# Pairing the second half's forget gate and query: two Strassen units, a seventh buffer pair, and scalings on ScalarE

## The chip, the core and the metric

The kernel runs on one core of a Trainium2 chip. The engines that matter here are PE (TensorE, the matmul engine; its weight loads are counted apart as PEld), DVE (VectorE), ACT (ScalarE), POOL (GpSimd) and SP (SyncE, whose queue issues the weight transfers). The metric is the device time of one execution in microseconds (us), as the median of several runs.

## The reference

A single layer of a hybrid block over 256 tokens of width 2048: a gated short convolution beside a gated linear recurrence with 8 heads of 128, a gated merge, an output projection and a per-token embedding gate, all in float32.

```python
h = rmsnorm(x, norm_mix_g[i])
u = h @ w_in[i]
c_g, b_g, xa, za, q, fl, iv, og, ga, gb = jnp.split(u, split_idx, axis=-1)
ya = b_g * causal_dwconv3(c_g * xa, conv_w[i]) * jax.nn.silu(za)
...
log_f = jnp.logaddexp(jnp.log(jnp.maximum(lb, LB_FLOOR)),
                      jnp.log1p(-lb) + jax.nn.log_sigmoid(flf))
kk = (1.0 - lb) * jax.nn.sigmoid(-flf)
o = hgrn2_chunked(jax.nn.silu(q), kk, iv, log_f)          # reshaped to heads
...
m = jax.nn.sigmoid(ga) * (ya @ w_a_out[i]) + jax.nn.sigmoid(gb) * (yb @ w_b_out[i])
x = x + m @ w_o[i]
gate = jax.nn.sigmoid(rmsnorm(x, ple_norm_g[i]) @ w_ple_gate[i])
x = x + gate * (p[i] @ w_ple_proj[i])
```

The column blocks `q`, `fl` (the forget gate, `f` in the kernel), `iv` and `og` are 1024 wide and belong to the recurrence. `log_f` equals the logarithm of `lb + (1 - lb) * sigmoid(fl)`; the kernel computes it so, per head, with `one` = 1 - lb and `low` = lb as per-partition columns, since features lie on the partitions there.

## The kernel before, in words

**Products.** Every float32 matmul is made of three products of a high and a low part: `x_hi w_hi + x_hi w_lo + x_lo w_hi`. The weights come in chunks of 128 x 1024 values, called positions here and numbered through the whole program (`pos`). For each position ACT makes the high part (`whi`, L166: a copy to the matmul type) and DVE the low part (`wlo`, L167: raw minus `whi`). PE then issues 12 products of 128 x 512. L1258 is the matmul of a plain group, L1280 that of a pair.

**Groups.** The program runs group after group; a group is a block of 512 output columns, and a block of 1024 input columns is handled as halves 0 and 1. For the first half: `f`, then `QV` (query and value as a pair), `og`, `c`, `xa`, `za`, `b`. For the second half: `f` at positions 72 to 79, `q` at 80 to 87, and `VG` (value and output gate as a pair) at 88 to 109, then `c`, `xa`, `za`, `b`. After that come the merge gates `G0` and `GG`, the branch projections `A` and `B`, the output projection (`OO`, a pair, then two plain groups `O`), and the gate of the embedding `PG`, `GP`. In all 342 positions.

**Pairs and units.** A pair makes two groups at once after a program such as `INNER`, a tuple of entries. `(g, c)` stands for two plain positions for group g, from k-chunk c on (`(2, c)` for one position each for both groups). `("S", c)` is a Strassen unit of four positions (parts 0 to 3) that need 6, 3, 6 and 6 products, 21 in place of 24. For a unit DVE forms sums of raw weights after part 0's split (`combine_weights`, L181, L184, L185; part 1 is then only 512 wide), and sums of inputs are kept as `form`s. Since a unit leaves its results in eight banks, the function `sums` adds these up to the two outputs (L845, after a copy by ACT, L858); it starts the work on the first output as soon as it is complete, then the second.

**What sets the order.** Each engine runs its instructions strictly in the program's order, which is that of the code. At each position PE's products are written, the casts and splits run ahead by `ahead(pos)` positions (LEAD = 3, and one more for each additional buffer pair where the rule in `ahead` allows it), and every active epilogue (a generator, such as `ep_f`) advances by one step: one step for each plain position, one for every second part of a unit. In the regions where extra pairs are named, further order constraints keep casts, splits and steps in that order.

**Buffers.** `whi` and `wlo` rotate through four pairs of the pool `wp`; in some regions of the program (`MORE`) there are one or two extra pairs, made of tiles that happen to be unused there. With n extra pairs a position takes an extra one where `pos % (4 + n) < n`, otherwise the next of the four. So a position's number decides which earlier position must be finished before its cast. Region "inner" has two extra pairs, around `QV` and around `VG`. Raw weights come by transfers of SP's queue, three buffers deep; `turned` turns a gate to the layout of features on partitions by way of DRAM and a transpose on DVE (L354).

**The forget gate.** `ep_f` takes the product of `f`, scales it (L362), turns it, takes two sigmoids on ACT (L400, L402), applies the per-head scalings on DVE (L407: times `one` plus `low`; L414: times `one`), four each per half, loads the table for the logarithm, takes logarithms (L424, L425, L428) and makes a running sum on DVE (the scan, L434); two short operations follow (L439, L440).

Of the kernel before, what the change touches and what calls it, by code (L numbers as in the profile page):

```python
# [40 lines left out]

GATES = ("S", 0), (0, 2), ("S", 1), (1, 2), ("S", 4), (0, 6), ("S", 5), (1, 6)
OPENING = (0, 2), (0, 4), ("S", 0), (0, 6), ("S", 1), (1, 2), (1, 4), (1, 6)
INNER = (0, 4), ("S", 0), (0, 6), ("S", 1), (2, 3), ("S", 2), (1, 4), (1, 6)
# [11 lines left out]
def hybrid_kernel(ctx, tc, xT, x, pT, prm, gfin, masks, w_in, w_a, w_b, w_o, w_pg, w_pp, out):  # L56
# [117 lines left out]
    def combine_weights(pos):  # L174

        b = load(pos).rearrange("p i (k c) -> p (i k) c", k=2)
        pool, tag, n = ("tmp2", "t2", 2) if more(pos) in ("gates", "last") else ("tmp3", "t2", 1)
        if more(pos) in ("inner", "first"):
            pool, tag, n = "tmp1", ("both", "aoff")[unit_of[pos] // 2 % 2], 1
        t2 = half[unit_of[pos]] = pools[pool].tile([P, CW], F32, tag=tag, bufs=n, name=nm("t2"))  # L180
        nc.vector.tensor_tensor(  # L181
            out=b[:, 0:4:3, :], in0=b[:, 0:3:2, :], in1=b[:, 3:4, :].to_broadcast([P, 2, CW]), op=ALU.subtract
        )
        nc.vector.tensor_tensor(out=t2, in0=b[:, 2, :], in1=b[:, 0, :], op=ALU.add)  # L184
        nc.vector.tensor_tensor(out=b[:, 1, :], in0=b[:, 1, :], in1=t2, op=ALU.subtract)  # L185
# [27 lines left out]
    for gi, (kind, j, w, g, op, *program) in enumerate(groups):  # L213
# [4 lines left out]
        for n, (u, c) in enumerate(program[0]):  # L218
# [10 lines left out]
    LEAD = 3  # L229
# [26 lines left out]
    inner = [of_kind(kind) for kind in ("QV", "VG")]  # L256
    inner = range(inner[0][0] - 3, inner[0][-1] + 1), range(inner[1][0] - 6, inner[1][-1] + 1)

    def more(pos):

        return "gates" if pos in gates else "last" if pos in last else "outer" if pos in outer else "first" if pos in g0 else "inner" if any(pos in at for at in inner) else None

# [132 lines left out]
    def ep_f(j, psum):  # L395
# [9 lines left out]
        for h in range(4):  # L405
            s = slice(h * T, (h + 1) * T)
            nc.vector.tensor_scalar(  # L407
                out=sg[:, s], in0=sg[:, s], scalar1=one[:, h : h + 1], scalar2=low[:, h : h + 1],
                op0=ALU.mult, op1=ALU.add,
            )  # L410
        yield
        for h in range(4):
            s = slice(h * T, (h + 1) * T)
            nc.vector.tensor_scalar(  # L414
                out=kT[:, s], in0=sn[:, s], scalar1=one[:, h : h + 1], scalar2=None, op0=ALU.mult
            )
        yield
# [484 lines left out]
    def ep_out(j, e, left):  # L902
# [6 lines left out]
        yield from sums(e, left, lambda: (t4(), t4()), then)  # L909

    def ep_a(j, psum):
        g = state["ga", j]
# [406 lines left out]
    for pos, (gi, c) in enumerate(steps[:last_group]):  # L1319
# [53 lines left out]
        if program:  # L1373
# [4 lines left out]
            if c == (min(n for n, (u, _) in enumerate(program) if u == "S"), 0) and kind not in ("G0", "OO"):  # L1378
                active.append({"GG": ep_pair, "GP": ep_gates_late, "QV": ep_inner, "VG": ep_inner}[kind](j, banks, left))
            pair_products(c, program, opname)  # L1380
# [160 lines left out]
```

## Time and profile before

| | |
|---|---|
| Time, median of 3 runs | 808.21 us (807.93 to 808.41) |
| Profiled execution: time, span | 809.07 us, 807.3 us |
| Granted TensorE clock, mean | 0.996 |
| PE busy | 99% of the span |
| DVE busy | 85% |
| ACT busy | 61% |
| POOL busy | 12% |

The profiled execution is one run of the program; the times quoted from timelines are microseconds from its span's start. A row of a timeline has start, duration, engine, line, operation, output and inputs, shapes and a count; in brackets how long the engine was idle before, and what released it. A row of the chain that ended last has start, duration, engine, output and line. With PE busy 99% of the span, a change can save at most the products that it removes and the few gaps, and it can add whatever time it makes PE wait.

### The profile page before, as it was taken

To read this page: it belongs to the slowest core of one execution; us is meant where nothing else is said; L and a number is where in the kernel's file an instruction comes from. 1 tells how busy PE (TensorE), PEld (TensorE's weight loads), DVE (VectorE), ACT (ScalarE), POOL (GpSimd) and SP (SyncE) were. 2 spreads that over 40 slices of the span, in tenths; PEclk is the share of its full clock that TensorE was granted. 3 is DMA by queue.
4 is the path that set the end of the run, shared out by engine and by line. 5 is a ranking of instruction groups with operands and counts; after the bars stand their busy time and mean duration, and the time that the engine had idled before them with its cause. 6 is when DMAs were issued, how large, how long until landed. Compare 5 with 4: busy or idle time off the path is not lost.

```text
span 807.3 us, 11113 instructions
## 1 busy us (share of the span) xinstructions
PE 798.0 (99%) x4169; PEld 662.3 (82%) x4169; DVE 685.1 (85%) x798; ACT 492.1 (61%) x662; POOL 95.4 (12%) x74
## 2 busy tenths in 40 slices
PE   9999999999999999999999999999999999999995
PEld 7888888888888888888888888888888888887885
DVE  5968897966779987978998998998998988859995
ACT  6967565575656665586674564564565556746562
POOL 0000145300000054300001000000100000002032
PEclk9999999999999999999999999999999999999998
DMA  9899855747676755667584775775875669877542
GB/s 345 295 335 319 268 174 203 237 167 241 240 261 190 261 183 201 209 211 257 189 307 158 227 275 171 239 264 179 275 266 196 208 246 348 327 236 281 205 173 104
DMA packets 50309, 191.20 MB, mean 237 GB/s; under 512 B 5712, under 2 KB 15184, under 8 KB 36304
## 3 DMA queue, kind: packets, MB, share of 16 engines
q1 hardware_dynamic: 50112, 190.24, 68.4%
q8 instruction: 32, 0.52, 0.2%
q10 hardware_dynamic: 144, 0.26, 0.1%
q14 instruction: 21, 0.17, 0.1%
HBM read 175.80 MB, written 14.68 MB: 236 GB/s over the span
## 4 chain that ended last, share of the span: by engine, by line
PE 82%; DVE 10%; issue 2%; DMA 2%; ACT 2%; SPq 0%; POOL 0%; ACTq 0%; POOLq 0%; DVEq 0%
PE g L1258 48%; PE g L1280 25%; PE s L1280 6%; DVE wlo L167 5%; DMA raw<-in_w_pg 2%; ACT whi L166 1%; DVE raw L181 1%; DMA raw<-in_w_o 1%; PE s L1258 1%; PE s L504 1%; DVE t L845 1%; PE s L1131 1%; DVE t L184 1%; DVE t L1017 0%; DVE t L354 0%
## 5 line engine op out<-in xcount | busy, mean ns | idle before, releaser
L167 DVE TENSOR_TENSOR wlo<-raw,whi 128x1024 fp32r<-128x1024 f32 (+1 forms) x320 | 390.2, 1243 | 92.2 <-ACT whi L166 89.4
L166 ACT ACTIVATE whi<-raw 128x1024 fp32r<-128x1024 f32 (+1 forms) x320 | 325.8, 1047 | 175.8 <-PE g L1258 98.3
L1258 PE MATMUL g<-whi,xl 128*128 128x512 f32 (+1 forms) x464 | 177.1, 382 | 0.3 <-DVE xl L311 0.3
L1258 PE MATMUL g<-whi,xh 128*128 128x512 f32 (+1 forms) x464 | 177.4, 383 | 0.0
L1258 PE MATMUL g<-wlo,xh 128*128 128x512 f32 (+1 forms) x464 | 177.1, 382 | 0.0
L1280 PE MATMUL g<-whi,xl 128*128 128x512 f32 x316 | 122.9, 389 | 0.0
L1280 PE MATMUL g<-wlo,xh 128*128 128x512 f32 x316 | 122.9, 389 | 0.0
L1280 PE MATMUL g<-whi,xh 128*128 128x512 f32 x316 | 122.6, 389 | 0.0
L1258 PEld LDWEIGHTS g<-whi,xl 128*128 128x128 f32 x464 | 87.2, 188 | 17.6 <-DVE xl L311 0.8
L1258 PEld LDWEIGHTS g<-whi,xh 128*128 128x128 f32 x464 | 87.2, 188 | 17.0 <-ACT xh L310 0.3
L1258 PEld LDWEIGHTS g<-wlo,xh 128*128 128x128 f32 x464 | 87.3, 188 | 16.8
L166 ACT ACTIVATE whi<-t 128x512 fp32r<-128x512 f32 x25 | 15.8, 632 | 92.1 <-DVE t L184 92.1
L1280 PEld LDWEIGHTS g<-whi,xl 128*128 128x128 f32 x316 | 59.3, 188 | 12.4
L1280 PEld LDWEIGHTS g<-whi,xh 128*128 128x128 f32 x316 | 59.3, 188 | 12.3
L1280 PEld LDWEIGHTS g<-wlo,xh 128*128 128x128 f32 x316 | 59.3, 188 | 12.3
L927 POOL TENSOR_TENSOR t<-ga,gb 128x512 f32<-128x512 f32 x6 | 10.6, 1790 | 188.0 <-issue 118.1
L181 DVE TENSOR_TENSOR raw<-raw 128x1024 f32<-128x1024 f32 x25 | 31.5, 1261 | 0.6
L1258 PE MATMUL g<-whi,yaTh 128*128 128x512 f32 (+1 forms) x74 | 28.2, 388 | 0.0
L1258 PE MATMUL g<-wlo,yaTh 128*128 128x512 f32 (+1 forms) x74 | 27.9, 383 | 0.0
L1258 PE MATMUL g<-whi,yaTl 128*128 128x512 f32 (+1 forms) x74 | 27.9, 383 | 0.0
L1258 PE MATMUL g<-whi,mh 128*128 128x512 f32 x64 | 24.8, 391 | 0.1
L1258 PE MATMUL g<-whi,ml 128*128 128x512 f32 x64 | 24.9, 389 | 0.0
(309 smaller groups left out, 1117.0 us busy)
## 6 DMA issues: line engine op xcount, KB each, us to landing
raw<-in_w_in SPq DMA_DIRECT2D x68, 1024.0 KB, 5.0
raw<-in_w_in SPq DMA_DIRECT2D x37, 512.0 KB, 5.1
raw<-in_w_o SPq DMA_DIRECT2D x12, 1024.0 KB, 6.5
raw<-in_w_pg SPq DMA_DIRECT2D x12, 1024.0 KB, 6.4
raw<-in_w_in SPq DMA_DIRECT2D x38, 256.0 KB, 5.1
turn<-t SPq DMA_DIRECT2D x72, 128.0 KB, 2.8
t<-turn SPq DMA_DIRECT2D x18, 512.0 KB, 5.2
raw<-in_w_a SPq DMA_DIRECT2D x8, 1024.0 KB, 5.6
```

The costliest lines, as they stand in the source:

```text
L166: a = nc.scalar.activation(out=hi[:, s], in_=src[:, s], func=AF.Copy)
L167: v = nc.vector.tensor_tensor(out=lo[:, s], in0=src[:, s], in1=hi[:, s].bitcast(F32), op=ALU.subtract)
L181: nc.vector.tensor_tensor(out=b[:, 0:4:3, :], in0=b[:, 0:3:2, :], in1=b[:, 3:4, :].to_broadcast([P, 2, CW]), op=ALU.subtract)
L184: nc.vector.tensor_tensor(out=t2, in0=b[:, 2, :], in1=b[:, 0, :], op=ALU.add)
L504: nc.tensor.matmul(heads(bk)[r, h, c if at is None else slice(at, at + 32)], key(h)[:, r], query(h)[:, c], start=True, stop=True, tile_pos ...
L845: nc.vector.tensor_tensor(out=out, in0=x, in1=y, op=ALU.add)
L927: (nc.vector if j == 3 else nc.gpsimd).tensor_tensor(out=spread(m, t), in0=blocks(ga[:, s]), in1=blocks(gb[:, s]), op=ALU.add)
L1131: nc.tensor.matmul(wb[:m, :n], *ones, start=True, stop=True)
L1258: nc.tensor.matmul(psum, a, b, start=first and n == 0, stop=last and n == 2)
L1280: nc.tensor.matmul(banks[name], x, y[:, s], start=k == total[name] and i == 0, stop=k == 1 and i == 2)
```

## The change

It does four things.

1. Groups `f` and `q` of the second half become a pair `FQ` with the program `SECOND`: six plain entries of two positions and two Strassen units, 20 positions (72 to 91) in place of 16. `ep_second` passes the first output to `ep_f` and the second to `ep_q`. `VG` moves to 92 to 113, and all later positions rise by four (the whole program has 346).
2. A new region "wide", from four positions before `VG` to its end, has a third extra pair made of the tiles `og` and `cv`, so seven pairs in all; `ahead` has a case for it. Region "inner" now reaches from two positions before `FQ` to the start of "wide".
3. In `ep_f` the eight scalings of each half leave DVE (L407, L414) and become activations on ACT (L415 with scale and bias as per-partition columns, L421 with a scale).
4. The input sums for `VG`'s third unit (`third`) start at a place counted from "wide".

Lines of the new kernel lie a little lower: L166 becomes L167, L167 becomes L168, L400 becomes L408, L845 becomes L850, L1280 becomes L1296.

```diff
+SECOND = (0, 2), (0, 4), ("S", 0), (0, 6), ("S", 1), (1, 2), (1, 4), (1, 6)
...
-        if more(pos) in ("inner", "first"):
+        if more(pos) in ("inner", "wide", "first"):
             pool, tag, n = "tmp1", ("both", "aoff")[unit_of[pos] // 2 % 2], 1
...
-        elif (kind, j) in (("iv", 0), ("og", 1)):
+        elif (kind, j) == ("f", 1):
+            groups.append(("FQ", j, w_in, n, "hT", SECOND))
+        elif (kind, j) in (("iv", 0), ("og", 1), ("q", 1)):
             continue
...
+        "wide": (
+            (("tmp1", "X"), ("tmp1", "X")), (("tmp1", "a"), ("tmp1", "y")), (("tmp1", "og"), ("tmp1", "cv")),
+        ),
...
-    inner = range(inner[0][0] - 3, inner[0][-1] + 1), range(inner[1][0] - 6, inner[1][-1] + 1)
+    wide = range(inner[1][0] - 4, inner[1][-1] + 1)
+    inner = range(inner[0][0] - 3, inner[0][-1] + 1), range(of_kind("FQ")[0] - 2, wide[0])
+    tied.append(wide)
...
-            nc.vector.tensor_scalar(
-                out=sg[:, s], in0=sg[:, s], scalar1=one[:, h : h + 1], scalar2=low[:, h : h + 1],
-                op0=ALU.mult, op1=ALU.add,
+            nc.scalar.activation(
+                out=sg[:, s], in_=sg[:, s], func=AF.Identity, scale=one[:, h : h + 1], bias=low[:, h : h + 1]
             )
...
-            nc.vector.tensor_scalar(
-                out=kT[:, s], in0=sn[:, s], scalar1=one[:, h : h + 1], scalar2=None, op0=ALU.mult
-            )
+            nc.scalar.activation(out=kT[:, s], in_=sn[:, s], func=AF.Identity, scale=one[:, h : h + 1])
...
+    def ep_second(j, e, left):
+
+        def then(q, g):
+            after = (ep_q if q else ep_f)(j, [g[:, A], g[:, B]])
             next(after)
             active.append(after)
+
+        yield from sums(e, left, lambda: (t4(), t4()), then)
...
-        while n < len(MORE[at]) and more(pos + LEAD + n + 1) == at and (at == "gates" or more(pos + LEAD - 2 * n) == at):
+        while n < len(MORE[at]) and more(pos + LEAD + n + 1) == at and (
+            at == "gates" or more(pos + LEAD - 2 * n) == at or at == "wide" and n < 2
+        ):
             n += 1
...
-        if pos == inner[1][0] - 8:
+        if pos == wide[0] - 10:
```

The order of instructions shows where things stand. On ACT, in the kernel before, the forget gate of the second half comes among the casts of `VG`'s first unit (`whi_2210` to `whi_2288` are its parts 0 to 3; L400 and L402 are the sigmoids, L370 a part of q's activation).

```order
L166 ACTIVATE whi_2210<-raw_2152 128x1024 [waits DMAHW4_49,DVE_49,PE_49]
L400 ACTIVATE t_367_2208<-t_366_2206 128x1024 [waits DMAHW6_49,DMAHW7_49,DMAHW1_49,DVE_49]
L402 ACTIVATE t_366_2206<-t_366_2206 128x1024 [waits Activation_49]
L166 ACTIVATE whi_2240<-t_370_2214 128x512 [waits DVE_49,PE_49]
L166 ACTIVATE whi_2260<-raw_2152 128x1024 [waits DVE_49,PE_49]
L370 ACTIVATE t_377_2276<-g_2115,r1r_615 128x512 [waits PE_49]
L370 ACTIVATE t_377_2276<-g_2116,r1r_615 128x512 [waits PE_49]
L166 ACTIVATE whi_2288<-raw_2152 128x1024 [waits DMAHW6_49,DMAHW5_49]
L424 ACT_TABLE_LOAD
L424 ACTIVATE t_385_2306<-t_367_2208 128x4x128 [waits DVE_49]
```

On ACT, in the changed kernel, the same work comes among the casts of `VG`'s second unit (`whi_2366` is its part 0, position 100; `whi_2385` to `whi_2404` are parts 1 to 3, and `whi_2422` is position 104).

```order
L167 ACTIVATE whi_2366<-raw_2264 128x1024 [waits DMAHW3_49,PE_49,Activation_49]
L408 ACTIVATE t_393_2304<-t_392_2302 128x1024 [waits DVE_49]
L378 ACTIVATE t_399_2327<-t_363_2141,r1r_615 128x512 x2
L410 ACTIVATE t_392_2302<-t_392_2302 128x1024 [waits Activation_49]
L415 ACTIVATE t_393_2304<-t_393_2304,lc_54_330,lc_55_331 128x256 x4
L421 ACTIVATE kT_2340<-t_392_2302,lc_55_331 128x256 [waits Activation_49]
L421 ACTIVATE kT_2340<-t_392_2302,lc_55_331 128x256 x3
L167 ACTIVATE whi_2385<-t_408_2370 128x512 [waits DVE_49,PE_49]
L167 ACTIVATE whi_2393<-raw_2264 128x1024 [waits DVE_49,PE_49]
L167 ACTIVATE whi_2404<-raw_2264 128x1024 [waits DMAHW6_49,DMAHW4_49,PE_49]
L429 ACT_TABLE_LOAD
L429 ACTIVATE t_421_2416<-t_393_2304 128x4x128 [waits Activation_49]
```

The batch has moved back by one unit and two plain entries, and the eight scalings have joined it, ahead of the casts of parts 1 to 3.

On DVE, in the changed kernel, the transpose of the forget gate (L362) follows the split of position 100 (`wlo_2367`), and the scan (L439) stands between the splits of 105 and 106.

```order
L168 TENSOR_TENSOR wlo_2367<-raw_2264,whi_2366 128x1024 [waits DMAHW3_49,Activation_49]
L362 STREAM_TRANSPOSE t_392_2302<-t_375_2197 128x4x8x32 [waits DMAHW5_49]
L182 TENSOR_TENSOR raw_2264<-raw_2264 128x2x512 [waits DMAHW6_49,DMAHW4_49,DVE_49]
...
L168 TENSOR_TENSOR wlo_2423<-raw_2324,whi_2422 128x1024 [waits DMAHW7_49,Activation_49]
L168 TENSOR_TENSOR wlo_2441<-raw_2324,whi_2440 128x1024 [waits DMAHW0_49,PE_49,Activation_49]
L439 SCALAR_TENSOR_TENSOR b_2456<-carry,t_421_2416 128x1024 [waits Pool_49]
L168 TENSOR_TENSOR wlo_2460<-raw_2381,whi_2459 128x1024 [waits DMAHW1_49,Activation_49]
...
L444 COPY tot_2457<-b_2456 128x4x2
L445 TENSOR_TENSOR tot_2457<-b_2456,lfl_2417 128x4x2
L362 STREAM_TRANSPOSE qT_2333<-t_400_2328 128x4x8x32 [waits DMAHW1_49]
L168 TENSOR_TENSOR wlo_2486<-raw_2381,whi_2485 128x1024 [waits Activation_49]
```

On DVE, in the kernel before, the scan (L434) stood one unit earlier: behind the splits of `VG`'s (0, 6) and of S1's part 0 (`wlo_2344`), ahead of S1's weight sums (L181).

```order
L167 TENSOR_TENSOR wlo_2314<-raw_2188,whi_2313 128x1024 [waits DMAHW7_49,Activation_49]
L167 TENSOR_TENSOR wlo_2333<-raw_2188,whi_2332 128x1024 [waits Activation_49]
L167 TENSOR_TENSOR wlo_2344<-raw_2230,whi_2343 128x1024 [waits DMAHW0_49,PE_49,Activation_49]
L434 SCALAR_TENSOR_TENSOR b_2359<-carry,t_385_2306 128x1024 [waits Pool_49]
L181 TENSOR_TENSOR raw_2230<-raw_2230 128x2x512 [waits DMAHW2_49,DMAHW1_49,DVE_49]
```

So the scan and the transposes of f and q have moved behind one more unit of `VG`.

On ACT at the start of the output projection `OO`, the kernel before casts parts 2 and 3 of the first unit (`whi_5564`, `whi_5585`) and the position behind them so:

```order
L166 ACTIVATE whi_5531<-t_976_5527 128x512 [waits DVE_49,PE_49,Activation_49]
L166 ACTIVATE whi_5564<-raw_5440 128x1024 [waits DVE_49,PE_49,Activation_49]
L166 ACTIVATE whi_5585<-raw_5440 128x1024 [waits DMAHW6_49,DMAHW5_49]
L166 ACTIVATE whi_5589<-raw_5489 128x1024 [waits DMAHW7_49,PE_49,Activation_49]
L784 ACTIVATE Sm_5608<-t_980_5551 128x512 [waits DVE_49]
```

and the changed kernel, at the same place with positions four higher, so:

```order
L167 ACTIVATE whi_5567<-t_992_5563 128x512 [waits DVE_49,PE_49,Activation_49]
L167 ACTIVATE whi_5600<-raw_5476 128x1024 [waits DVE_49,PE_49,Activation_49]
L167 ACTIVATE whi_5621<-raw_5476 128x1024 [waits DMAHW1_49,DMAHW2_49,PE_49,Activation_49]
L167 ACTIVATE whi_5625<-raw_5525 128x1024 [waits DMAHW3_49]
L789 ACTIVATE Sm_5644<-t_996_5587 128x512 [waits DVE_49]
```

The same five instructions stand in the same order, but their buffers have rotated: the cast of part 3 now waits for PE, and the cast behind it does not.

More of the change, by code (lines that the diff above doesn't have):

```diff
@@ L256, in hybrid_kernel @@
     inner = [of_kind(kind) for kind in ("QV", "VG")]
-    inner = range(inner[0][0] - 3, inner[0][-1] + 1), range(inner[1][0] - 6, inner[1][-1] + 1)
+    wide = range(inner[1][0] - 4, inner[1][-1] + 1)
+    inner = range(inner[0][0] - 3, inner[0][-1] + 1), range(of_kind("FQ")[0] - 2, wide[0])
+    tied.append(wide)
     def more(pos):
-        return "gates" if pos in gates else "last" if pos in last else "outer" if pos in outer else "first" if pos in g0 else "inner" if any(pos in at for at in inner) else None
+        return "gates" if pos in gates else "last" if pos in last else "outer" if pos in outer else "first" if pos in g0 else "wide" if pos in wide else "inner" if any(pos in at for at in inner) else None
     TOKENS, NORM, FORMS, MASKS = 10, 13, 5, 30
@@ L909, in ep_out @@
         yield from sums(e, left, lambda: (t4(), t4()), then)
+    def ep_second(j, e, left):
+        def then(q, g):
+            after = (ep_q if q else ep_f)(j, [g[:, A], g[:, B]])
+            next(after)
+            active.append(after)
+        yield from sums(e, left, lambda: (t4(), t4()), then)
     def ep_a(j, psum):
@@ L1378, in hybrid_kernel @@
             if c == (min(n for n, (u, _) in enumerate(program) if u == "S"), 0) and kind not in ("G0", "OO"):
-                active.append({"GG": ep_pair, "GP": ep_gates_late, "QV": ep_inner, "VG": ep_inner}[kind](j, banks, left))
+                active.append({"GG": ep_pair, "GP": ep_gates_late, "QV": ep_inner, "VG": ep_inner, "FQ": ep_second}[kind](j, banks, left))
             pair_products(c, program, opname)
```

## The prediction

> **What bounds the kernel now.** I read the page's first part, the chain that ended last, the table of windows around the change, and then the timelines of PE, ScalarE (ACT) and VectorE (DVE) there.
>
> ```profile
> PE 798.0 (99%) x4169; PEld 662.3 (82%) x4169; DVE 685.1 (85%) x798; ACT 492.1 (61%) x662; POOL 95.4 (12%) x74
> ```
> ```profile
> 177.53 62.58 PE g L1258 x276
> ...
> 240.10 5.44 PE g L1280 x24
> ```
> ```profile
> 200.00:220.00 20.00, 20.00 (x90) 16.54 (x90) 14.75 (x19) 11.15 (x16) 0.11 (x1) 1.00 0.78 270
> 240.00:260.00 20.00, 20.00 (x90) 16.57 (x89) 18.05 (x24) 13.79 (x18) 0.53 (x1) 1.00 0.49 158
> 260.00:280.00 20.00, 19.97 (x89) 16.21 (x88) 19.28 (x21) 12.56 (x15) 0.00 (x0) 1.00 0.74 263
> ```
>
> PE is full, so only two things change the time: the number of products, and stretches in which PE is left without a split weight. One product takes 62.58 / 276 = 0.2267 us. In the windows (length; then PE, PEld, DVE, ACT, POOL; granted clock; DMA share; GB/s) DVE has 5 us to spare at 200 to 220, 2.0 at 240 to 260, 0.7 at 260 to 280. DVE is the second bound exactly where the changed groups hand over to VG. VG starts at 240.10; FQ's 20 positions need 6 products less than the 16 of f and q, so after the change VG would start at 240.10 - 1.36 = 238.74.
>
> ```profile
> 268.05 0.39 PE L1280 MATMUL g<-whi,xh 128*128 128x512 f32 x1
> ...
> 268.80 0.39 PE L1280 MATMUL s<-whi,form 128*128 128x512 f32 x1
> ```
>
> These two starts are two products apart and should differ by 0.45, not 0.75: PE already loses 0.30 us in VG's third unit, S2.
>
> **The change, part by part.** *Products.* One unit has 21 in place of 24, so two save 6: -1.36 us. The 0.30 of S2 goes too, since what follows counts S2's delay from its nominal place.
>
> *The gate batch, moved into VG.* Before, f's last product runs at 177.53 + (84 + 96) x 0.2267 = 218.3 (7 and 8 positions of 12), and the work on its gates stands among the casts of VG's first unit S0, 6 to 12 us before PE reaches them (S0 starts at 240.10 + 5.44 = 245.54):
>
> ```profile
> 235.75 1.06 ACT L400 ACTIVATE t<-t 128x1024 f32<-128x1024 f32 x1 [1.00 <-DMA raw<-in_w_in]
> ...
> 241.31 1.24 ACT L370 ACTIVATE t<-g,r1r 128x512 f32<-128x512 f32 x2
> ...
> 243.52 1.28 ACT L424 ACT_TABLE_LOAD   x1
> 244.81 0.63 ACT L424 ACTIVATE t<-t 128x512 f32<-128x512 f32 x1
> ...
> 245.97 2.94 ACT L166 ACTIVATE whi<-raw 128x1024 fp32r<-128x1024 f32 x3
> ```
> ```profile
> L407 DVE TENSOR_SCALAR t<-t,lc,lc x8: 406/408/414, 77.9 to 240.2; 128x256 f32<-128x256 f32 x8
> L414 DVE TENSOR_SCALAR kT<-t,lc x8: 334/348/555, 81.5 to 241.9; 128x256 f32<-128x256 f32 x8
> L434 DVE TENSOR_TENSOR_SCAN b<-carry,t x2: 2276/2280/2283, 87.4 to 250.5; 128x1024 f32<-128x1024 f32 x2
> ```
> ```profile
> 205.75 1.69 ACT L310 ACTIVATE ybTh<-t,prm_t 128x256 fp32r<-128x256 f32 x4
> ```
>
> As a pair, f is complete only after both units (114 products from 196.57: 222.4), its sums take adds on DVE, and the steps behind them are counted in positions. In ACT's new order sigmoids, scalings and logarithms stand between whi of VG's S1 part 0 (position 100) and whi of (2,3) (104); on DVE the transpose stands behind the split of 100. The eight scalings leave DVE (4 x 0.41 + 4 x 0.35, about 3 us) and join this queue at L310's 1.69 / 4 = 0.42 less overlap, 0.40 each: 3.2 us. They stand in front of the casts 101 to 104, so DVE waits behind ACT and PE behind both.
>
> From the transpose's end to the start of whi 104, ACT has: sigmoid 0.97 (1.06 less 0.09 overlap), silu pair 1.24, sigmoid 0.97, scalings 3.2, half cast 0.63, casts 102 and 103 at 2.94 / 3 = 0.98, table load 1.29, logarithms 245.97 - 244.81 = 1.16: 11.42 us.
>
> What DVE does next is priced from a unit of another pair:
>
> ```profile
> 390.26 1.22 DVE L167 TENSOR_TENSOR wlo<-raw,whi 128x1024 fp32r<-128x1024 f32 x1
> 391.51 1.23 DVE L181 TENSOR_TENSOR raw<-raw 128x1024 f32<-128x1024 f32 x1
> ...
> 394.25 0.69 DVE L167 TENSOR_TENSOR wlo<-t,whi 128x512 fp32r<-128x512 f32 x1
> 395.40 2.36 DVE L167 TENSOR_TENSOR wlo<-raw,whi 128x1024 fp32r<-128x1024 f32 x2 [0.46 <-ACT whi L166]
> 397.68 1.24 DVE L354 STREAM_TRANSPOSE t<-t 128x1024 f32<-128x1024 f32 x1
> ...
> 408.10 0.68 DVE L845 TENSOR_TENSOR gb<-gb,s 128x512 f32<-128x512 f32 x1
> 408.70 1.22 DVE L167 TENSOR_TENSOR wlo<-raw,whi 128x1024 fp32r<-128x1024 f32 x1
> ```
> ```profile
> 247.05 3.50 DVE L167 TENSOR_TENSOR wlo<-raw,whi 128x1024 fp32r<-128x1024 f32 x3 [1.36 <-ACT whi L166]
> ...
> 257.67 0.17 DVE L439 COPY tot<-b 128x8 f32<-128x8 f32 x1
> ```
>
> A unit takes 397.68 - 390.26 = 7.42 us, its part 0 with the combining 394.25 - 390.26 = 3.99. After whi 104 starts: cast 1.06, splits 104 and 105 at 1.15, scan 2.21, part 0 of S2 3.99, its half split 0.62, copy 0.17, q's transpose 1.17, split 108 1.22 = 12.74. So position 108 is ready 24.2 us after the transpose ends. PE needs it 28.11 us after VG's start (2 x 2.72, a unit 4.76, 2 x 2.72, a unit 4.76, 2 x 2.72, and 6 + 3 products 2.04 = 27.88, plus 0.23 until the lo part): at 266.85.
>
> When does the transpose end? Two bounds. Buffers:
>
> ```profile
> 605.59 8.17 PE g L1258 x36
> 613.85 1.07 ACT whi L166
> ```
>
> A cast starts 0.09 after its buffer's last product. Whi 100 takes the seventh pair, which the second position of (0,4) frees at 238.74 + 5.44 + 0.16 (the last product's tail) = 244.34: cast until 245.5, split 246.6, transpose until 247.8. Position 108 is then ready at 272.0, 5.1 us late. Backlog: the last time that DVE must wait is FQ's S1, whose part 0 is cast after whi 81 (its pair is freed at 207.7 by the position that ends at 196.57 + 4 x 2.72 = 207.45) and four ybTh (1.69), so its split starts at 211.6. From there to the transpose DVE's order holds two units 14.84, eleven splits 12.65, one transpose 1.17, three full adds 3.5, seven half adds at 0.60 (408.10 to 408.70) 4.2, four small rows 0.8 (an estimate, 0.2 each by the copy's 0.17): 37.2. The transpose ends at 249.9 and 108 is ready at 274.1, **7.2 us late**. I take the backlog, since it is the later of two conditions that must both hold. The wait falls in pieces at 101 to 104 and in S2, the largest about 1.9 us. DVE's idle waits would add to it: one like the row at 247.05 is 1.36.
>
> *The scalings on another engine* are 3.2 of these 7.2 us on ACT and take 3 off DVE. The Trainium skill, "ScalarE: Activation LUTs", "Rules for kernel authors", sends adds and multiplications to VectorE; its "What ACT_TABLE_LOAD costs" adds 93 ns for each pointer operand. By L310 with one pointer my 0.40 holds; L415 with two would be 0.09 longer by that page, 0.37 more for four, and the result 815.6.
>
> *The first half's scalings* move too.
>
> ```profile
> 80.93 54.40 PE g L1258 x240
> ```
> ```profile
> 83.47 2.00 ACT L166 ACTIVATE whi<-raw 128x1024 fp32r<-128x1024 f32 x2
> ```
>
> Delayed 3.2 us, the first of these two casts ends at 87.7 and its split at 88.9; it is position 35, which PE needs at 80.93 + 3 x 2.72 + 0.23 = 89.3. It just fits: 0, at most +0.5.
>
> *FQ's own units* are covered by DVE's 5 us in 200 to 220 less the saved scalings; buffers are freed 7.5 us or more ahead there. 0, at most one late cast, +1.0.
>
> *Four more positions* shift the rotation of the buffer pairs for all later groups. By the release order only OO changes for the worse: the cast of S0's part 3 waited for no PE; now its pair is the one that (0,4)'s second position reads, whose last product is the one before this:
>
> ```profile
> 632.63 0.39 PE L1280 MATMUL s<-whi,mh 128*128 128x512 f32 x1
> ```
>
> ```profile
> 627.66 2.01 ACT L166 ACTIVATE whi<-raw 128x1024 fp32r<-128x1024 f32 x2
> ```
> ```profile
> 632.55 2.35 DVE L167 TENSOR_TENSOR wlo<-raw,whi 128x1024 fp32r<-128x1024 f32 x2
> ...
> 653.52 6.90 DVE L167 TENSOR_TENSOR wlo<-raw,whi 128x1024 fp32r<-128x1024 f32 x6 [0.46 <-ACT whi L166]
> ```
> ```profile
> 658.18 6.59 DMA raw<-in_w_o
> ...
> 669.58 42.93 PE g L1258 x188
> ```
>
> That cast ran as the second at 628.6; now it starts at 632.88 (632.63 + 0.16 for the product's tail + 0.09) and its split at 633.98, where DVE had begun the first of two at 632.55: 1.43 later. DVE then has no pause until 653.52, where some 0.5 is spare, and the raw load at 658.18, released by the splits, ends at the PE wait before 669.58, which passes on the rest. Bounds 0.5 and 1.43; with two places that both pass it on, I take **+1.4**.
>
> SP's queue: f's gates go through memory ahead of VG's raw loads; the load for S1 then lands around 244.5, before it is read. POOL's rows stay.
>
> **Sum**, on the profiled run: 809.07 - 1.36 - 0.30 + 7.2 + 1.4 = 816.0. That run lies 0.86 above the median, so 815.2. Own range: 815.2 - 2.1 (buffer bound) - 0.9 (OO at 0.5) = 812.2 to 815.2 + 0.5 + 1.0 + 1.36 = 818.1.
>
> **Rivals.** *Faster.* The seven pairs let ACT and DVE run further ahead: if the transpose ends by 242.7 (266.85 - 24.2), nothing waits and OO's wait may be absorbed too: 808.21 - 1.66 = 806.5. For it speaks the 5 us of DVE's spare time in 200 to 220; against it that even the buffer bound gives 247.8, so S1's part 0 would have to be split before the transpose without a free pair. Chance 0.08. *Same.* VG holds, but OO's 1.4 eats the saved products: 808.0. The same evidence; 0.12. *The clock drops in VG's gaps.*
>
> ```profile
> 795.00:800.00 5.00, 4.21 (x36) 4.00 (x34) 2.69 (x10) 1.41 (x3) 0.55 (x1) 1.00 0.55 210
> 800.00:803.60 3.60, 0.00 (x0) 0.00 (x0) 2.31 (x7) 1.34 (x2) 0.54 (x1) 0.68 0.15 53
> ```
>
> PE ends near 799.2; a mean of 0.68 over 3.6 us means full clock for 1.3 us and half after, so the clock halves about 2.1 us into the idle time. A gap of 1.9 is close; one unit at half clock would add 21 x 0.2267 = 4.8: 820.0. Chance 0.06. The Trainium skill, "TensorE: Matmul & The Clock Gate", Part 1, gives an idle window of about 3.4 us; by that none of these gaps would do it, and by the 2.1 of the rows here only one grown by 0.2.
>
> **Numbers.** Forecast 0.74, faster 0.08, same 0.12, clock 0.06. A difference under 0.2% (1.6 us) can't be told from none; 806.5 lies just beyond. The range 808.0 to 818.1 leaves out the faster rival, half of the same, and the clock. Slower 0.80, within 0.2% 0.12, faster 0.08; predicted 815.2.
>
> **What would show it.** Right: windows 240 to 280 with PE short by about 7 us; weight loads in 255 to 275 that wait for whi and wlo; the ACT timeline with eight 0.40 scalings and a table load between whi of S1 and of (2,3); in OO's first unit a whi released by PE and its wlo 1.4 later against PE than in the rows above. Wrong: PE full there, which means that the transpose came early; a stall in FQ at 196 to 240 or at 89, which means those covers were gone; a clock under 1.00 in the windows; the wait before 669.58 unchanged, which means OO's delay found slack.

## The result, and the profile after

The changed kernel takes 814.46 us (median of 4 runs, 813.34 to 815.34) beside 808.31 us for the kernel before (4 runs, 807.93 to 808.67). The ratio is 1.0075 (95% interval 1.0058 to 1.0093): it is slower by 6.15 us, where 7.0 were forecast. The profiled execution took 813.34 us with a span of 811.5 us, so it is the fastest of the four, 1.1 us below their median; the profiled execution before (809.07 us) was 0.8 us above the median given here.

The head of the page, for the changed kernel:

```profile
span 811.5 us, 11133 instructions
...
PE 798.3 (98%) x4162; PEld 660.1 (81%) x4163; DVE 693.7 (85%) x799; ACT 501.7 (62%) x683; POOL 94.9 (12%) x74
```

Nothing of this tells where the time went. The windows do (length; busy time of PE, PEld, DVE, ACT and POOL; granted clock; DMA share; GB/s):

```profile
240.00:260.00 20.00, 18.64 (x80) 14.49 (x79) 15.45 (x18) 15.59 (x23) 0.53 (x1) 1.00 0.59 188
260.00:280.00 20.00, 17.48 (x71) 12.32 (x70) 17.71 (x19) 11.18 (x15) 0.00 (x0) 1.00 0.59 208
```

PE, full in both windows before, now lacks 1.4 and 2.5 us, and DVE lacks work too: it idles 4.6 and 2.3 us. In what follows "gaps" are the time between the starts of successive products, less the 0.227 us of one product, summed. That counts more than PE's idle time does: a product's row lasts 0.39 us and overlaps the next, so a late start need not leave PE idle. From 240 to 280 the gaps are 6.45 us, before 0.30.

ACT's timeline there holds the whole batch of the forget gate in a row:

```profile
249.38 1.06 ACT L408 ACTIVATE t<-t 128x1024 f32<-128x1024 f32 x1 [4.17 <-DVE t L362]
250.34 1.32 ACT L378 ACTIVATE t<-t,r1r 128x512 f32<-128x512 f32 x2
251.57 1.04 ACT L410 ACTIVATE t<-t 128x1024 f32<-128x1024 f32 x1
252.52 2.06 ACT L415 ACTIVATE t<-t,lc,lc 128x256 f32<-128x256 f32 x4
254.49 1.69 ACT L421 ACTIVATE kT<-t,lc 128x256 f32<-128x256 f32 x4
256.08 0.61 ACT L167 ACTIVATE whi<-t 128x512 fp32r<-128x512 f32 x1
256.60 1.99 ACT L167 ACTIVATE whi<-raw 128x1024 fp32r<-128x1024 f32 x2
258.62 1.28 ACT L429 ACT_TABLE_LOAD   x1
...
261.07 2.94 ACT L167 ACTIVATE whi<-raw 128x1024 fp32r<-128x1024 f32 x3
269.89 0.63 ACT L167 ACTIVATE whi<-t 128x512 fp32r<-128x512 f32 x1 [5.89 <-DVE t L185]
```

ACT idles 4.17 us ahead of it, because DVE's transpose comes late, and then the casts of S1's parts 1 to 3 (256.08, 256.60) and of (2,3) (261.07) stand behind it. DVE's timeline shows who waits for that:

```profile
248.10 1.24 DVE L362 STREAM_TRANSPOSE t<-t 128x1024 f32<-128x1024 f32 x1
...
256.73 0.69 DVE L168 TENSOR_TENSOR wlo<-t,whi 128x512 fp32r<-128x512 f32 x1 [3.74 <-ACT whi L167]
257.68 2.36 DVE L168 TENSOR_TENSOR wlo<-raw,whi 128x1024 fp32r<-128x1024 f32 x2 [0.26 <-ACT whi L167]
262.14 2.36 DVE L168 TENSOR_TENSOR wlo<-raw,whi 128x1024 fp32r<-128x1024 f32 x2 [2.10 <-ACT whi L167]
264.42 2.29 DVE L439 TENSOR_TENSOR_SCAN b<-carry,t 128x1024 f32<-128x1024 f32 x1
...
272.48 6.86 DVE L168 TENSOR_TENSOR wlo<-raw,whi 128x1024 fp32r<-128x1024 f32 x6
```

So DVE, the second bound, loses 6.1 us (3.74 + 0.26 + 2.10) behind ACT's queue, and the split of position 108 starts at 272.48 and ends at 273.7 (the forecast said 274.1). PE's weight loads wait in three places, in S1, at (2,3) and in S2:

```profile
256.75 0.19 PEld L1296 LDWEIGHTS s<-whi,yaTh 128*128 128x128 f32 x1 [1.55 <-ACT whi L167]
...
262.16 0.30 PEld L1296 LDWEIGHTS g<-whi,xh 128*128 128x128 f32 x2 [1.31 <-ACT whi L167]
...
270.57 0.19 PEld L1296 LDWEIGHTS s<-whi,form 128*128 128x128 f32 x1 [1.21 <-ACT whi L167]
```

The last of these waits is for the half cast at 269.89, which itself waited for DVE's sums (L185): by then DVE was late with the time that it had lost before.

From the two profiles, the spans differ by 4.2 us: -1.36 for the products, +6.15 in VG, +0.24 in OO and just behind it (gaps of 0.58 between 640 and 690, before 0.34), +0.13 at the start, and -0.83 for a gap that the profile before has near 730 us and this one has not. That is +4.33. The medians differ by 6.15; the other 1.9 us are how far the two profiled executions lie from their medians, and no profile shows where they go.

### The profile page after: what moved, and what is told of

It is laid out like the page before. It is cut to its first block, busy times and chain, and to the rows that moved or that the text cites. A ratio compares the mean times of both kernels' runs of the same rounds, so it can differ in the third digit from the quotient of the medians.

```text
span 811.5 us, 11133 instructions
## 1 busy us (share of the span) xinstructions
PE 798.3 (98%) x4162; PEld 660.1 (81%) x4163; DVE 693.7 (85%) x799; ACT 501.7 (62%) x683; POOL 94.9 (12%) x74
## 4 chain that ended last, share of the span: by engine, by line
PE 80%; DVE 11%; ACT 3%; issue 3%; DMA 2%; SPq 0%; POOL 0%; ACTq 0%; POOLq 0%; DVEq 0%
PE g L1274 44%; PE g L1296 27%; PE s L1296 6%; DVE wlo L168 4%; ACT whi L167 2%; DMA raw<-in_w_pg 1%; DVE raw L182 1%; DVE t L850 1%; DVE t L185 1%; PE s L1274 1%; PE s L509 1%; DVE t L1031 1%; PE s L1145 1%; DMA raw<-in_w_in 1%; DVE raw L186 0%
## 5 line engine op out<-in xcount | busy, mean ns | idle before, releaser
L168 DVE TENSOR_TENSOR wlo<-raw,whi 128x1024 fp32r<-128x1024 f32 (+1 forms) x322 | 393.5, 1247 | 78.7 <-ACT whi L167 77.4
L167 ACT ACTIVATE whi<-raw 128x1024 fp32r<-128x1024 f32 (+1 forms) x322 | 326.8, 1047 | 159.0 <-PE g L1274 81.4
L1274 PE MATMUL g<-wlo,xh 128*128 128x512 f32 (+1 forms) x400 | 152.3, 381 | 0.0
L1274 PE MATMUL g<-whi,xh 128*128 128x512 f32 (+1 forms) x400 | 152.2, 382 | 0.0
L1274 PE MATMUL g<-whi,xl 128*128 128x512 f32 (+1 forms) x400 | 152.1, 381 | 0.0
L1296 PE MATMUL g<-whi,xh 128*128 128x512 f32 x368 | 143.0, 390 | 1.3 <-ACT whi L167 1.3
L1296 PE MATMUL g<-wlo,xh 128*128 128x512 f32 x368 | 143.2, 389 | 0.0
L1296 PE MATMUL g<-whi,xl 128*128 128x512 f32 x368 | 143.2, 389 | 0.0
L1274 PEld LDWEIGHTS g<-whi,xh 128*128 128x128 f32 x400 | 75.2, 188 | 14.3
L1296 PEld LDWEIGHTS g<-whi,xh 128*128 128x128 f32 x368 | 68.9, 188 | 16.7 <-ACT whi L167 2.6
L1296 PEld LDWEIGHTS g<-whi,xl 128*128 128x128 f32 x368 | 69.1, 188 | 14.5
L1296 PEld LDWEIGHTS g<-wlo,xh 128*128 128x128 f32 x368 | 69.1, 188 | 14.4
L167 ACT ACTIVATE whi<-t 128x512 fp32r<-128x512 f32 x27 | 17.1, 632 | 99.0 <-DVE t L185 99.0
L182 DVE TENSOR_TENSOR raw<-raw 128x1024 f32<-128x1024 f32 x27 | 34.0, 1258 | 0.7
L1274 PE MATMUL g<-whi,ybTh 128*128 128x512 f32 x64 | 24.9, 389 | 0.0
```

The costliest lines, as they stand in the source:

```text
L167: a = nc.scalar.activation(out=hi[:, s], in_=src[:, s], func=AF.Copy)
L168: v = nc.vector.tensor_tensor(out=lo[:, s], in0=src[:, s], in1=hi[:, s].bitcast(F32), op=ALU.subtract)
L182: nc.vector.tensor_tensor(out=b[:, 0:4:3, :], in0=b[:, 0:3:2, :], in1=b[:, 3:4, :].to_broadcast([P, 2, CW]), op=ALU.subtract)
L1274: nc.tensor.matmul(psum, a, b, start=first and n == 0, stop=last and n == 2)
L1296: nc.tensor.matmul(banks[name], x, y[:, s], start=k == total[name] and i == 0, stop=k == 1 and i == 2)
```

## Experiments

Two theories stood against each other. By the first, ACT's queue and the place of the batch in it make the gaps: DVE and PE wait because the casts stand behind the gate's work. By the second, DVE simply has too much to do up to position 108, and it doesn't matter where the batch stands. Each run is given with its time, its ratio to the kernel before on the same chip (with a 95% interval), and the gaps from 240 to 280 us.

**The changed kernel again.** No edit.

> The changed kernel once more, for a second profile and as a companion of the other runs: 813.3 to 815.4 us, as in its four runs, with 6.0 to 7.0 us of gaps between products in VG (its profile showed 6.45, before 0.30). Its runs differ by 2 us where those of the kernel before differ by 0.7. If the gaps in VG vary from run to run, this profile shows others there; if the late raw loads near 730 us vary, the gap of 0.83 us that the kernel before has there is back.

It took 813.77 us (813.29 to 814.22), before 808.48 (ratio 1.0064, 1.0049 to 1.0079). The gaps are 6.45 again and there is none near 730. So VG's gaps don't vary between these two profiles.

**The second half's scalings back on DVE.**

```diff
-            nc.scalar.activation(out=sg[:, s], in_=sg[:, s], func=AF.Identity, scale=..., bias=...)
+            if j:
+                nc.vector.tensor_scalar(out=sg[:, s], in0=sg[:, s], scalar1=..., scalar2=..., op0=ALU.mult, op1=ALU.add)
...
```

> The changed kernel with the eight scalings of the second half back on DVE. Theory one, ACT's queue sets the gaps (DVE idles 3.7, 0.3 and 2.1 us behind ACT's casts at 253 to 262): the casts of VG's S1 come 3.7 us earlier, DVE does its 3.0 us of scalings in time that it now idles, position 108 is ready some 3 us earlier, VG's gaps fall to about 3.5 us, and the time to about 811.5. Theory two, DVE's backlog sets them: 3.0 us more of DVE work, gaps of 9 to 9.5 us, 817.5.

812.69 us (ratio to before 1.005, 1.0035 to 1.0065), gaps of 5.36: 1.1 less, between the two theories and nearer to the first. The timeline tells why. DVE took the scalings into its order ahead of a sum that the cast of part 1 needs (L185):

```profile
253.71 1.13 DVE L428 TENSOR_SCALAR kT<-t,lc 128x256 f32<-128x256 f32 x4
254.76 0.68 DVE L185 TENSOR_TENSOR t<-raw 128x512 f32<-128x512 f32 x1
...
257.36 2.36 DVE L168 TENSOR_TENSOR wlo<-raw,whi 128x1024 fp32r<-128x1024 f32 x2 [0.46 <-ACT whi L167]
261.81 2.36 DVE L168 TENSOR_TENSOR wlo<-raw,whi 128x1024 fp32r<-128x1024 f32 x2 [2.10 <-ACT whi L167]
```

That cast then waited for DVE, where before DVE had waited for it (ACT's row):

```profile
255.53 0.63 ACT L167 ACTIVATE whi<-t 128x512 fp32r<-128x512 f32 x1 [2.19 <-DVE t L185]
```

The later wait of 2.10 behind the table load stayed.

**The second half's scalings left out** (its gates are then plain sigmoids).

```diff
-        nc.scalar.activation(out=sn, in_=sn, func=AF.Sigmoid, scale=-1.0)
+        nc.scalar.activation(out=kT if j else sn, in_=sn, func=AF.Sigmoid, scale=-1.0)
...
-        for h in range(4):
+        for h in range(0 if j else 4):
```

> The changed kernel without the second half's eight scalings at all: the gates are taken as plain sigmoids there, so that part of the computation is left out. Theory one, ACT's queue: 3.7 us less in front of the casts, gaps of about 2.7 us, 810.7. Theory two, DVE's backlog: DVE's work is that of the changed kernel, so the gaps stay at 6 to 6.5 and the time at 814.5. Against the run with the scalings on DVE this prices them there: 0 if DVE does them in idle time, 3 if not.

809.8 us (1.0021, 1.0011 to 1.0031), gaps of 3.05. The first theory had said 2.7 and 810.7; the second 6 to 6.5 and 814.5. DVE's work is the same as in the changed kernel, so its amount alone does not make the gaps. The eight scalings cost 3.4 us of gaps on ACT (6.45 less 3.05) and 2.3 on DVE (5.36 less 3.05), and 3.05 remain without them.

**The lag after the turn, 2 in place of 4.**

```diff
-        sn = yield from turned(fl, 4 if j else 6)
+        sn = yield from turned(fl, 2 if j else 6)
```

> The changed kernel with the second half's forget gate taken up two steps sooner after its way through memory (a lag of 2 in place of 4), so that transpose, sigmoids, scalings and logarithms come ahead of VG's S1 part 0 on ACT. No work is taken away. Theory one, ACT's queue: the batch falls into the 4.2 us in which ACT idled ahead of it, the casts of S1 come 3 to 4 us sooner, gaps of 2.5 to 3.5 us, 810.5 to 811.5. Theory two, DVE's backlog: DVE's total up to position 108 is the same, gaps and time unchanged, 814.5. A third way: the transfer through memory has not landed, DVE waits for it ahead of its splits, and the time rises above 815.

814.11 us (1.0069, 1.0054 to 1.0084), gaps of 6.87: by the numbers the second theory, but the edit did not do what it was made for, so the run decides nothing between the two. The transpose kept its place behind the split of position 100, and the table load and the logarithms moved, in front of S1's casts (ACT, then DVE):

```profile
256.08 1.28 ACT L429 ACT_TABLE_LOAD   x1
...
258.53 0.61 ACT L167 ACTIVATE whi<-t 128x512 fp32r<-128x512 f32 x1
```
```profile
248.00 1.24 DVE L362 STREAM_TRANSPOSE t<-t 128x1024 f32<-128x1024 f32 x1
```

So the description of the kernel, by which an engine's order is that of the code, is too simple: where no constraint forbids it, the builder may put an instruction later on its engine than the code has it. The casts of S1 now stand behind still more of the batch, the first of them at 258.53 where the changed kernel has 256.08. Some 1.7 us of the 6.87 are a drop of PE's clock, told at the end.

**The transpose held ahead of the splits.** The splits after its step must follow it on DVE.

```diff
+        turn = nc.vector.transpose(...)
+        if first:
+            state["splits"] = (*state["splits"], turn.ins)
...
-        sn = yield from turned(fl, 4 if j else 6)
+        sn = yield from turned(fl, 4 if j else 6, first=j)
```

> The changed kernel with one order constraint more: the splits that follow the step with the forget gate's transpose stay behind it, so that DVE's order has it ahead of the splits of 98 to 100, 3.4 us sooner (the edit of the lag had left it in its place). Theory, ACT's queue and the place of the batch: ACT idled 4.2 us ahead of it, the whole batch comes 3 to 3.5 us sooner, gaps of 3 to 3.5 us, 810.5 to 811. Rival, DVE's backlog: DVE has the same work up to position 108, gaps 6 to 6.5, 814. If the transfer through memory has not landed by 244, DVE waits for it and the gaps grow.

811.24 us (1.003, 1.002 to 1.004), gaps of 3.36, in the first theory's range; its time is just above it. No work was removed; the same batch began 3.2 us sooner:

```profile
244.92 1.25 DVE L362 STREAM_TRANSPOSE t<-t 128x1024 f32<-128x1024 f32 x1
```
```profile
246.20 1.06 ACT L410 ACTIVATE t<-t 128x1024 f32<-128x1024 f32 x1 [0.86 <-DVE t L362]
```

ACT's idle time ahead of the batch fell from 4.17 to 0.86 us, and nearly all of that, 3.1 us, came off the gaps.

**Six pairs in place of seven.**

```diff
         "wide": (
-            (("tmp1", "X"), ("tmp1", "X")), (("tmp1", "a"), ("tmp1", "y")), (("tmp1", "og"), ("tmp1", "cv")),
+            (("tmp1", "X"), ("tmp1", "X")), (("tmp1", "a"), ("tmp1", "y")),
         ),
```

> The changed kernel without the seventh buffer pair (region wide has the two extra pairs of inner). Theory, the gaps come from the forget gate's batch on ACT and its place: VG's S1 part 0 is cast at most 1.5 us later, still ahead of the transpose, so gaps of 6.5 to 8 us, 814 to 815.5. Rival, the lead of seven pairs is what keeps the gaps this small: gaps of 9 us or more, 817 or more. If seven pairs do nothing: unchanged.

814.74 us (1.0077, 1.0052 to 1.0103), gaps of 7.08. The seventh pair is worth some 0.6 us of gaps in these profiles, and not the 3 or more of the rival; in the times the difference lies inside the spread.

**The scalings on ACT in the kernel before**, and nothing else of the change.

> The kernel before with the sixteen scalings on ACT and nothing else changed. Theory, the scalings cost only where the batch stands close ahead of PE: in the kernel before it stands among the casts of VG's S0, 6 to 12 us ahead, DVE gets 3 us back, so 807.5 to 808.5, gaps in VG between 0 and 0.6. Rival, each microsecond on ACT costs PE 0.9 as in the changed kernel (gaps 6.45 with them, 3.05 without): 811.5. The prediction's term for the first half (0, at most 0.5) shows here at 80 to 95 us.

809.11 us beside 808.45 (ratio 1.0001, 0.9991 to 1.0012): no difference that can be told. The gaps from 240 to 280 are 0.61. The same eight instructions that cost 3.4 us of gaps in the changed kernel cost 0.3 here (0.61 less the 0.30 of the kernel before), where the batch stands 6 to 12 us ahead of PE.

**The batch behind the units.**

```diff
-        sn = yield from turned(fl, 4 if j else 6)
+        sn = yield from turned(fl, 12 if j else 6)
```

> The changed kernel with the second half's forget gate taken up eight steps later (a lag of 12 in place of 4), behind VG's S2 on ACT and DVE. Theory, the place of the batch: the casts of S1 and S2 follow each other without it, position 108 is ready at about 264, ahead of PE's need at 266.9, so no gaps in VG; but the batch then stands in front of the casts at VG's end and in c, where the lead is 1 to 3 us: gaps of 1 to 4 us there, 808.5 to 811.5. Rival, DVE's total work is what counts: the gaps only move, 6 us in all, 814.

808.11 us beside 808.45 (0.9993, 0.9983 to 1.0003). There are no gaps in VG at all; 0.58 us appear later, in the groups behind it. The window of VG's second half and the batch on ACT:

```profile
250.00:280.00 30.00, 30.00 (x134) 24.82 (x133) 26.32 (x28) 24.14 (x33) 0.58 (x2) 1.00 0.66 230
```
```profile
267.67 1.04 ACT L408 ACTIVATE t<-t 128x1024 f32<-128x1024 f32 x1
...
273.72 1.28 ACT L429 ACT_TABLE_LOAD   x1
```

The same work, 18 us later on ACT, costs PE at most these 0.58 us there. The second theory, by which the gaps only move, is refuted. The edit moves DVE's part of the batch as well (the transpose and the scan, 3.5 us), so this run tells of the place of the batch; that the queue of ACT makes the gaps is told by the run without scalings, in which DVE's work did not change.

**The late batch with the old rotation of buffers**, to measure the prediction's second term.

```diff
-        if pos % (4 + n) < n:
-            places = [... MORE[more(pos)][pos % (4 + n)]]
+        at = pos - 4 * (pos > 120)
+        if at % (4 + n) < n:
+            places = [... MORE[more(pos)][at % (4 + n)]]
```

> The run with the batch behind the units, and the four additional positions taken out of the rotation: behind position 120 the choice of buffer pairs goes by the position less 4, as in the kernel before. It tells the prediction's second term: OO +1.4. Theory by the profiles so far: in the run with the late batch the split of OO's part 3 has 0.83 us to spare where the kernel before has 2.26, 1.43 later as predicted, but the gaps in OO are only 0.55 us, and those near 669 us are 0.3 in both; so 0.4 to 0.7 us less here, 807.5. Rival, the prediction's own size: 1.4 less, 806.7. Third, nothing, if other waits take the place: 808.1.

807.32 us beside 808.32 (0.9988, 0.9979 to 0.9997): 1.0 below the kernel before, where the late batch alone is 0.3 below it. By the medians that is 0.7 less, within the theory by the profiles, but the intervals of the two ratios overlap, so the times alone don't settle it. The profiles do for OO. In the profile of the late batch with the shifted rotation, ACT waits for PE in OO, and DVE waits behind it:

```profile
631.91 2.01 ACT L167 ACTIVATE whi<-raw 128x1024 fp32r<-128x1024 f32 x2 [4.15 <-PE g L1296]
```
```profile
633.00 2.36 DVE L168 TENSOR_TENSOR wlo<-raw,whi 128x1024 fp32r<-128x1024 f32 x2 [1.33 <-ACT whi L167]
```

With the old rotation the gaps between 640 and 690 us go from 0.88 to 0. Of these, 0.58 are in OO's last unit; the other 0.30 lie near 669 us, where the kernel before has 0.34 with the old rotation too, so that they are the rotation's is not shown.

**All scalings back on DVE, with the late batch and the old rotation.**

> The run before this one with all sixteen scalings back on DVE. If the scalings on ACT are a gain where the batch has room (DVE has 3 us less per half): 0.5 to 2 us slower than the run before, since DVE's backlog in VG and c grows. If they are neither gain nor loss: the same within 0.4. If ACT's queue in front of c's first casts is what is left (0.2 to 0.5 us of gaps there): up to 0.5 faster.

806.31 us beside 808.32: ratio 0.9976 (0.9966 to 0.9987), faster than both kernels, and 1.0 faster than with the scalings on ACT. Its expectation had the sign wrong, or half the size in its third case. Where the batch has room, DVE does the eight scalings in 2.4 us while ACT goes on (DVE's rows, then the window):

```profile
269.18 1.37 DVE L417 TENSOR_SCALAR t<-t,lc,lc 128x256 f32<-128x256 f32 x4
270.47 1.14 DVE L429 TENSOR_SCALAR kT<-t,lc 128x256 f32<-128x256 f32 x4
```
```profile
250.00:280.00 30.00, 30.00 (x134) 24.86 (x133) 29.26 (x35) 21.36 (x25) 0.58 (x2) 1.00 0.67 229
```

In that profile the gaps are 0 from 60 to 130, 240 to 314 and 640 to 666 us, and 0.03 from 666 to 690; with the scalings on ACT they were 0.91 from 60 to 130 us and 0.59 from 280 to 314. The first of these varies from profile to profile (below), and the profiled execution with the scalings on ACT was 1.0 us above its median, so how the 1.0 us between the medians divides is not shown.

**A lag of 10 in place of 12.**

> The late batch with the old rotation, taken up two steps sooner (lag 10 in place of 12), so that the sigmoids and scalings come among the casts of VG's S2 on ACT. By the theory of the place, S2 has 1.5 to 3 us to spare there and the eight scalings take 3.7: gaps of 1 to 3 us in S2 are back, 808.5 to 810.5. If only DVE's work counted: unchanged against lag 12.

811.77 us (1.0045, 1.0031 to 1.0059), gaps of 4.34, more than expected. The batch stands among the casts of S2, and two steps of lag decide 4.4 us (807.32 against 811.77). Some 1.7 us of the gaps are the clock, below; the rest is inside the range that was expected.

## Why the prediction was right

**Products:** right. From the first product of the pair to VG's start the forecast had 42.17 us (238.74 less 196.57); in the profile after it is 42.16 (196.30 to 238.46).

**The gate batch in VG, 7.2 us:** right in place, chain and nearly in size, 6.45 us of gaps. The transpose was put at 248.8 and came at 248.10. The scalings were put at 3.2 us and took 3.56 (252.52 to 256.08). The two errors nearly cancel, which is luck: whi 104 was forecast for 261.3 and came at 261.07. Of the two bounds, the one by DVE's backlog was the right one to take for the transpose: from the split at 211.26 (forecast 211.6) to the transpose DVE has only two pauses, 0.44 and 0.47 us. The prediction had DVE wait behind ACT after that, but did not say how long: it is 6.1 us, so the backlog sets the beginning of the batch and ACT's queue its cost. The run without scalings, the one with the transpose held ahead and the late batch show that. With the transpose held ahead, the prediction's own chain (24.2 us from the transpose's end at 246.17) puts position 108 at 270.4, 3.5 us late, and the gaps are 3.36.

**The scalings' price:** undersized by 0.36 us. From start to start, a step with a scale alone takes 0.40 us (254.49 to 256.08 for four), as the prediction had it; with a second pointer, the bias, it takes 0.49 (252.52 to 254.49). The single durations in ns (least, mean, most) are:

```profile
L415 ACT ACTIVATE t<-t,lc,lc x8: 584/586/590, 77.6 to 254.0; 128x256 f32<-128x256 f32 x8
...
L421 ACT ACTIVATE kT<-t,lc x8: 492/493/495, 80.1 to 255.7; 128x256 f32<-128x256 f32 x8
```

The difference is 93 ns. That is the figure for a pointer operand in the Trainium skill, "ScalarE: Activation LUTs", "What ACT_TABLE_LOAD costs", which the prediction weighed and did not take. The rule of the Trainium skill, "ScalarE: Activation LUTs", "Rules for kernel authors", that multiplications belong on VectorE agrees with the pair of runs that differ in this alone: 806.31 us with the scalings on DVE, 807.32 with them on ACT.

**The first half, 0 to +0.5:** the bound was too small. In the eleven profiles of kernels with these scalings on ACT the gaps from 60 to 130 us are 0 in six and 0.15, 0.16, 0.31, 0.80 and 0.91 in the others; the two largest have their largest gap at 89.7 and 89.4 us, where the prediction had found that it just fits (89.3). In the two profiles with the scalings on DVE they are 0; two are few.

**FQ's own units, 0:** right, no gap from 195 to 240 us in any run.

**OO, +1.4:** the term was too large, and the step that failed is that two places "both pass it on". The delay itself was as forecast: the split of OO's part 3 ends 0.83 us before PE reaches that part in the late batch (634.23 against 635.06), and 2.27 in the kernel before (633.76 against 636.03), 1.44 less. It then reaches OO's last unit undiminished. The splits whose row stands at 653.52 in the prediction begin at 653.98 in the late batch, behind the same pause, while PE runs 0.97 us sooner there:

```profile
653.98 6.90 DVE L168 TENSOR_TENSOR wlo<-raw,whi 128x1024 fp32r<-128x1024 f32 x6 [0.46 <-ACT whi L167]
```

In that unit only 0.58 us of it became gaps (at 654.9 in the late batch, 660.7 in the changed kernel). The prediction had looked for room in DVE's pauses alone (there is another one of 0.46 before, at 641.70, which it overlooked and which gave nothing back either). What it missed is what PE had in hand: in the kernel before, part 2's low half is split 0.54 us ahead of its product (654.75 against 655.29), and in the late batch two products that need no low half stand ahead of that product. Behind the unit the delay dies out, since these splits are 1.14 us apart and PE takes 2.72 for a position. The second place, the raw load at 658.18 and PE's wait before 669.58, passed on nothing: the gap there is 0.34 in the kernel before, 0.30 in the late batch and none in the changed kernel. In the profiles of before and after the term is +0.24.

**The sum.** Worked out on the profiled runs it said +6.9 (816.0 less 809.07) where the two profiles differ by 4.3: VG too large by 0.75 (7.2 against 6.45), OO by 1.2, and a gap of 0.83 near 730 us that went without having been in the sum. That it came as near to the median as it did (815.2 against 814.46) is partly luck: the profiled execution after was 1.1 us below the median of its runs. The gap near 730 us stands in the profiles of the two kernels with the old positions (0.83 and 0.60) and in none of the others; its cause was not tried.

**The rivals.** "Faster" needed the transpose to end by 242.7; it ended at 249.34, and at 246.17 even when it was held ahead, and the seventh pair is worth only 0.6 us. "Same" needed VG to hold, and VG lost 6.15. "The clock drops in VG's gaps" did not happen in the changed kernel, whose largest distance between starts is 1.5 us (clock 1.00 in both windows above), but it did in two of the experiments, with waits of 2.4 and 3.7 us.

## What to carry to other kernels

Here, removing six products is worth 1.36 us, and the same edit cost 6 by moving another stage's epilogue in front of casts that have little lead: before pairing two groups, look where the epilogue behind them lands on the cast engine, and how far ahead of the matmul engine it stands there. Price a moved operation by its place: the same eight scalings cost 0.3 us of gaps where the casts were 6 to 12 us ahead and 3.4 where they were not. A later or an earlier place can then cure it with no work taken away (808.11 and 811.24 us, where the changed kernel takes about 814), and the new place has to be checked in the order of instructions, since a step in the code may leave an instruction where it was. With the batch behind the units, the old rotation and the scalings on DVE, the kernel with the pair is 2.0 us faster than the kernel before.

## What was not expected of the hardware

The clock. In the run with a lag of 10, PE waited once for 2.4 us, and the products after it ran at half speed for a while (PE's timeline, then windows with the granted clock as the third number from the end):

```profile
266.37 0.40 PE L1297 MATMUL s<-whi,form 128*128 128x512 f32 x1
269.16 0.80 PE L1297 MATMUL s<-whi,form 128*128 128x512 f32 x1 [2.40 <-ACT whi L168]
...
271.13 0.63 PE L1297 MATMUL s<-wlo,form 128*128 128x512 f32 x1
271.56 0.63 PE L1297 MATMUL s<-whi,form 128*128 128x512 f32 x1
```
```profile
268.00:269.00 1.00, 0.00 (x0) 0.00 (x0) 0.00 (x0) 1.00 (x2) 0.00 (x0) 0.94 0.00 0
269.00:270.00 1.00, 0.84 (x2) 0.50 (x2) 0.86 (x1) 1.00 (x3) 0.00 (x0) 0.50 0.00 0
...
272.00:273.00 1.00, 1.00 (x5) 0.86 (x4) 0.37 (x1) 1.00 (x2) 0.00 (x0) 0.85 0.58 106
```

If the clock is 1 and then a half, a mean of 0.94 means that it halved at 268.88, 2.1 us after the last product had ended (266.77), and 0.85 that it came back at 272.3: 3.4 us at half speed, with product starts 0.43 apart. In the run with a lag of 2 a wait of 3.68 us did the same, but later:

```profile
259.20 0.50 PE L1296 MATMUL s<-whi,yaTh 128*128 128x512 f32 x1 [3.68 <-ACT whi L167]
```
```profile
259.00:261.00 2.00, 1.58 (x5) 0.86 (x5) 1.57 (x2) 2.00 (x4) 0.53 (x1) 0.91 0.48 135
261.00:263.00 2.00, 2.00 (x5) 1.30 (x5) 2.00 (x3) 2.00 (x4) 0.00 (x0) 0.50 0.00 0
263.00:265.00 2.00, 2.00 (x8) 1.59 (x7) 2.00 (x2) 0.88 (x1) 0.00 (x0) 0.73 0.74 188
```

By the same reckoning it halved at 260.64, 1.4 us after PE had begun again, and came back at 264.1: 3.4 us once more. At half speed PE loses about half of that, the 1.7 us named above. So the clock does not drop at a fixed time after the last product, as the prediction took it from the end of the program (2.1 us): here it is 5.1, and at the end of the program 2.1 to 4.9 in the thirteen profiles. A wait of 2.4 us is enough.

The traces' records of the clock say more. Between two changes, the time at full clock is a whole multiple of 3.413 us in every profile (75 and 159 times that in the run with a lag of 2, 77 and 156 with a lag of 10), so the changes lie on a grid that runs through. Laid over PE's rows, each stretch of the grid that ended in a drop held at least 2.06 us without a product, and no stretch that left the clock at 1 held more than 1.72. This is worked out from thirteen profiles, with ends of products that are modelled. The Trainium skill, "TensorE: Matmul & The Clock Gate", Part 1, describes a free-running window of about 3.4 us that sees whether PE was busy; the durations at half speed and the grid agree with that. That one whole such window must be idle before the clock drops, as its table says, does not agree: 2.06 to 2.3 us of idle time in a window sufficed in several profiles.
